# LoRA matmul on one core: the first load moved up in the load queue, and the first store held until most of the first loads have landed

## The chip, the cores and the metric

The kernel runs on one core of one Trainium2 chip. The metric is the device time of one execution in microseconds (us); of several executions the median is taken. A profiled execution also has a span, the time from its first to its last recorded instruction, and its own device time, which is a little longer than the span.

## The reference

`x` has 32768 rows of 256 float32 numbers (a batch of 16 by 2048), `W` is 256 x 256, and the adapter has rank 16. What is computed is

```python
x_flat = x.reshape(-1, in_dim)
y = x_flat @ W
lora_out = x_flat @ lora_A      # 256 x 16
lora_out = lora_out * lora_E    # 16 numbers
lora_out = lora_out @ lora_B    # 16 x 256
y = y + scale * lora_out        # float32, shape of x
```

`x` is 33.6 MB and is read once; the output is as large and is written once. Everything else is small: `W` 256 KB, `lora_A` and `lora_B` 16 KB each, `lora_E` 64 bytes.

## The kernel before

The adapter is folded into the weights once: `weff = W + A diag(E * scale) B`, in bfloat16, and then every row of `x` is multiplied by `weff` alone.

**Chunks and the ring.** `PLAN` cuts the rows into seven chunks of 16, 32, 48, 48, 32, 48 and 32 blocks of 128 rows (a block is 128 KB of `x`, so 2, 4 and 6 MB a chunk). In SBUF they live in `xy`, a ring of `RING` = 176 blocks. The first five chunks (`LEAD`) fill the ring exactly. A chunk's result is written over its own rows in the ring and stored from there, so chunk 5 can be loaded only when the stores of chunks 0 and 1 have landed, and chunk 6 only when that of chunk 2 has.

**SyncE (SP)** issues every transfer of the kernel, on one queue, in an order written out by hand: `W`, `lora_A`, chunk 0, `lora_B`, `lora_E`, chunks 1 to 4 (lines 120 to 126), then chunk by chunk the stores (line 129), each as soon as `s_rdy` says that the chunk is computed. Behind the store of chunk 2 it waits for the stores named in `owners` (line 132) and issues the loads of chunks 5 and 6. At the end it waits for the stores.

**VectorE (DVE)** first makes `ate` (line 170) and `weff` (line 176), then takes the chunks in pieces of 16 blocks: it waits for the chunk's load (`s_in`), casts the piece to bfloat16 (line 184) and copies the transposed blocks from PSUM to SBUF (line 188, twice a piece). At the first piece of chunk `PAUSE` = 4 it also waits until the store of chunk 2 has landed:

```python
            if r == 0 and i == PAUSE:
                dve.wait_ge(s_out[again - 1], 16)
```

`again` is 3 here, so it is the store of chunk 2. The last six evictions of PSUM are VectorE's too (line 154).

**TensorE (PE)** transposes `lora_A` (line 216), multiplies `ate` by `lora_B` (line 220), and waits for `weff` (line 223). Then it loops over the 16 pieces: transposes (line 197), products with `weff` (line 205). **ScalarE (ACT)** evicts the products from PSUM into the ring (line 154) and raises `s_rdy` at the end of a chunk. **GpSimd (POOL)** makes the identity matrix, casts `lora_B` (line 145) and passes on one semaphore per chunk.

Of the kernel before, what the change touches and what calls it, by code (L numbers as in the profile page):

```python
# [6 lines left out]

PLAN = [16, 32, 48, 48, 32, 48, 32]  # L10

RING = 176

LEAD = 5
AFTER = {2: [5, 6]}

PAUSE = 4

# [6 lines left out]
def kernel(  # L25
# [20 lines left out]
    KC = K // P  # L46
    CHUNKS = len(PLAN)
    assert K == M == KC * P and sum(PLAN) * P == N and all(b % G == 0 for b in PLAN)

    def sbuf(name, shape, dt):  # L50
        return ctx.enter_context(nc.sbuf_tensor(name, shape, dt))

    def psum(name, shape, dt):
# [6 lines left out]
    w_sb = sbuf("w_sb", [P, KC, M], FP32)  # L60
    a_sb = sbuf("a_sb", [P, KC, R], FP32)
    b_sb = sbuf("b_sb", [R, M], FP32)
    e_sb = sbuf("e_sb", [R, 1], FP32)
    b_bf = sbuf("b_bf", [R, M], BF16)
    ate = sbuf("ate", [R, KC, P], BF16)
    weff = sbuf("weff", [P, KC, M], BF16)
# [5 lines left out]
    ps_at = ps_y[0][:R, 0, :].rearrange("r (c p) -> r c p", c=KC)  # L72
    ps_aeb = ps_y[1][:, :KC, :]

    sem = tc.alloc_semaphore
    s_w, s_a, s_b, s_e = sem("s_w"), sem("s_a"), sem("s_b"), sem("s_e")
    s_in = [sem(f"s_in{i}") for i in range(CHUNKS)]
    starts = [sum(PLAN[:i]) for i in range(CHUNKS)]
    places = [r % RING for r in starts]
    assert sum(PLAN[:LEAD]) <= RING and all(r + b <= RING for r, b in zip(places, PLAN))  # L80

    owners = {
        i: [j for j in range(LEAD) if places[j] < places[i] + PLAN[i] and places[i] < places[j] + PLAN[j]]
        for i in range(LEAD, CHUNKS)
    }
# [4 lines left out]
    s_lora = sem("s_lora")  # L90
    s_lpe = sem("s_lpe")
# [7 lines left out]
    def rows_of(flat, i):  # L99
        b, r0 = PLAN[i], starts[i] * P  # L100
        return flat[r0:r0 + b * P, :].rearrange("(p b) k -> p b k", b=b)

    def ring_of(i):
        return xy[:, places[i]:places[i] + PLAN[i], :]


    def pieces(rows):
        return [(i, r) for i, b in enumerate(PLAN) for r in range(0, b, rows)]

    def rows_at(i, r, rows):  # L110
        return xy[:, places[i] + r:places[i] + r + rows, :]

    with tc.tile_critical(sync_engine=mybir.EngineType.SP, no_gpsimd_drain=True):  # L113
        sp, pe, dve, act, pool = nc.sync, nc.tensor, nc.vector, nc.scalar, nc.gpsimd


        def load(i):
            sp.dma_start(out=ring_of(i), in_=rows_of(x_flat, i)).then_inc(s_in[i], 16)

        sp.dma_start(out=w_sb[:], in_=W.rearrange("(p c) m -> p c m", c=KC)).then_inc(s_w, 16)  # L120
        sp.dma_start(out=a_sb[:], in_=lora_A.rearrange("(p c) r -> p c r", c=KC)).then_inc(s_a, 16)
        load(0)
        sp.dma_start(out=b_sb[:], in_=lora_B).then_inc(s_b, 16)
        sp.dma_start(out=e_sb[:], in_=lora_E[:, None]).then_inc(s_e, 16)
        for i in range(1, LEAD):
            load(i)
        for i in range(CHUNKS):
            sp.wait_ge(s_rdy, i + 1)
            sp.dma_start(out=rows_of(out_flat, i), in_=ring_of(i)).then_inc(s_out[min(i, again)], 16)
            for later in AFTER.get(i, []):  # L130
                for j in owners[later]:
                    sp.wait_ge(s_out[j], 16)
                load(later)
        for i in range(len(s_out) - 1):
            sp.wait_ge(s_out[i], 16)


        pool.memset(ident[:], 0.0).then_inc(s_id, 1)  # L138
        pool.wait_ge(s_id, 1)
        pool.affine_select(  # L140
            out=ident[:], in_=ident[:], compare_op=mybir.AluOpType.not_equal, fill=1.0,
            base=0, pattern=[[-1, P]], channel_multiplier=1,
        ).then_inc(s_id, 1)
        pool.wait_ge(s_b, 16)
        pool.tensor_copy(out=b_bf[:], in_=b_sb[:]).then_inc(s_lora, 1)  # L145

        copies = pieces(Q)

        def y_of(q, engine, copy):
            i, r = copies[q]
            engine.wait_ge(s_p, q + 1)
            done = copy(out=rows_at(i, r, Q), in_=ps_y[q % 2][:])  # L154
            if r + Q == PLAN[i]:
                done.then_inc(s_rdy, 1)
            else:
                done.then_inc(s_y[q % 2], 1)

        for i in range(CHUNKS - 1):  # L160
            pool.wait_ge(s_rdy, i + 1).then_inc(s_y[((starts[i] + PLAN[i]) // Q - 1) % 2], 1)


        for q in range(len(copies) - LATE):
            y_of(q, act, act.copy)


        dve.wait_ge(s_e, 16)
        dve.wait_ge(s_lpe, 1)
        dve.tensor_scalar(  # L170
            out=ate[:], in0=ps_at, scalar1=e_sb[:], scalar2=float(scale),
            op0=mybir.AluOpType.mult, op1=mybir.AluOpType.mult,
        ).then_inc(s_lora, 1)
        dve.wait_ge(s_w, 16)
        dve.wait_ge(s_lpe, 2)
        dve.tensor_add(out=weff[:], in0=w_sb[:], in1=ps_aeb).then_inc(s_lora, 1)  # L176

        for g, (i, r) in enumerate(pieces(G)):
            if r == 0:
                dve.wait_ge(s_in[i], 16)  # L180
            if r == 0 and i == PAUSE:
                dve.wait_ge(s_out[again - 1], 16)

            dve.tensor_copy(out=xb[:], in_=rows_at(i, r, G)).then_inc(s_xb, 1)  # L184
            for k in range(g * G // S, (g + 1) * G // S):

                dve.wait_ge(s_t, k + 1)
                dve.tensor_copy(  # L188
                    out=xt[k % 2][:].rearrange("w j p c -> w j (p c)"), in_=ps_xt[k % 2][:].bitcast(BF16),
                ).then_inc(s_xt, 1)  # L190
        for q in range(len(copies) - LATE, len(copies)):
            y_of(q, dve, dve.tensor_copy)


        def transposes(k):
            for j in range(S):
                t = pe.transpose(ps_xt[k % 2][:, j, :], xb[:, k * S + j, :].bitcast(FP32), ident[:])  # L197
            t.then_inc(s_t, 1)

        def products(k):  # L200
            for h in range(S // Q):
                pe.wait_ge(s_y[h], 1).then_inc(s_y[h], -1)  # L202
                for j in range(Q):
                    for c in range(KC):
                        m = pe.matmul(  # L205
                            ps_y[h][:, j, :], xt[k % 2][:, h * Q + j, :, c], weff[:, c, :],
                            start=(c == 0), stop=(c == KC - 1),
                        )
                m.then_inc(s_p, 1)

        for h in range(2):
            pe.sem_inc(s_y[h], 1)
        pe.wait_ge(s_a, 16)
        pe.wait_ge(s_id, 2)
        for c in range(KC):
            t = pe.transpose(ps_at[:, c, :], a_sb[:, c, :], ident[:])  # L216
        t.then_inc(s_lpe, 1)
        pe.wait_ge(s_lora, 2)
        for c in range(KC):
            m = pe.matmul(ps_aeb[:, c, :], ate[:, c, :], b_bf[:], start=True, stop=True)  # L220
        m.then_inc(s_lpe, 1)

        pe.wait_ge(s_lora, 3)
        with pe.Fori(0, sum(PLAN) // G):
            pe.wait_ge(s_xb, 1).then_inc(s_xb, -1)  # L225
            for k in range(G // S):
                transposes(k)
            for k in range(G // S):
                pe.wait_ge(s_xt, 1).then_inc(s_xt, -1)
                products(k)  # L230
# [39 lines left out]
```

## Time and profile before

| | |
|---|---|
| median of 3 runs | 165.87 us (165.84, 165.87, 166.8) |
| the profiled execution, its own time | 165.25 us |
| its span | 163.5 us |
| its mean granted TensorE clock | 0.89 |
| TensorE busy (matmul) | 97.1 us, 59% of the span |
| VectorE busy | 81.7 us, 50% |
| ScalarE busy | 57.2 us, 35% |
| bytes moved | 67.42 MB, 412 GB/s over the span |
| time in the packets of SP's queue, as a share of the 16 DMA engines | 96.7% |

Times in the profile are microseconds from the start of the span. The profiled execution took 1.75 us more than its span (165.25 less 163.5), and this part is the same for all that follows. Its own time lies 0.6 us below the median of the runs. The table by stretches gives, for each stretch of the span, the busy time of the engines, then the granted TensorE clock, the share of time that the DMA engines were busy and the rate in GB/s. A packet is one partition's part of a transfer, up to 48 KB; in a stretch of one or two microseconds the rate is coarse, because a whole packet is booked in one place and the share can then pass 1.

### The profile page before, as it was taken

Reading aid. Unit: us, or ns where it says so; the run is one execution under the profiler, and the core shown is the slowest. Engines: PE = TensorE matmul, PEld = TensorE weight load, DVE = VectorE, ACT = ScalarE, POOL = GpSimd, SP = SyncE. Lnnn points to the kernel's source line nnn. Section 1 sums busy time; section 2 is a strip of 40 time slices with the busy share of each in tenths; the row PEclk is TensorE's granted clock in tenths of the full one; section 3 lists DMA queues with packets and bytes.
Section 4 is the critical chain, followed back from the end, with each engine's and each line's share of the span. In section 5 each row is a group of like instructions: output and inputs, shape, how many; then the busy total and the mean of one; then the engine's idle time right before and its main releaser. Section 6 shows DMA issues by size and latency. Waiting matters only on the chain. (4 is left out here: it accounts for less than half of the span.)

```text
span 163.5 us, 1907 instructions
## 1 busy us (share of the span) xinstructions
PE 97.1 (59%) x772; PEld 79.6 (49%) x772; DVE 81.7 (50%) x56; ACT 57.2 (35%) x59; POOL 1.1 (1%) x7
## 2 busy tenths in 40 slices
PE   0014998868978979886000698889789893810000
PEld 0004776747757767674000667677577672600000
DVE  0025768557494684850002484864946849730000
ACT  3000265490844737549000026648457420000000
POOL 1000000000000000000000000000000000000000
PEclk9999999999999999999755569999999998796555
DMA  5999999899999989999999998999998999999991
GB/s 140 401 461 449 449 457 409 385 481 457 409 417 401 377 361 457 457 445 409 457 457 421 397 481 389 425 449 425 469 445 361 457 433 437 493 397 401 425 409 48
DMA packets 2370, 67.42 MB, mean 412 GB/s; under 512 B 432, under 2 KB 448, under 8 KB 576
## 3 DMA queue, kind: packets, MB, share of 16 engines
q1 hardware_dynamic: 2368, 67.40, 96.7%
q14 instruction: 2, 0.02, 0.0%
HBM read 33.85 MB, written 33.55 MB: 412 GB/s over the span
## 5 line engine op out<-in xcount | busy, mean ns | idle before, releaser
L154 ACT COPY xy<-ps_y 128x1024 f32<-128x1024 f32 x58 | 56.0, 1016 | 73.7 <-PE ps_y L205 73.7
L205 PE MATMUL ps_y<-weff,xt 128*128 128x256 bf16 x512 | 64.2, 279 | 16.9 <-PEq L202 16.9
L205 PEld LDWEIGHTS ps_y<-weff,xt 128*128 128x128 bf16 x512 | 48.0, 100 | 32.5 <-issue 24.5
L188 DVE COPY xt<-ps_xt 128x2048 bf16<-128x2048 bf16 x32 | 37.9, 1220 | 32.3 <-PE ps_xt L197 32.3
L184 DVE CAST xb<-xy 128x4096 bf16<-128x4096 f32 x16 | 36.6, 2286 | 18.2 <-DMA out_dram<-xy 15.8
L197 PE MATMUL ps_xt<-ident,xb 128*128 128x128 f32 x256 | 34.1, 292 | 19.1 <-PEq L225 19.1
L197 PEld LDWEIGHTS ps_xt<-ident,xb 128*128 128x128 f32 x256 | 31.4, 151 | 20.3 <-issue 20.1
L154 DVE COPY xy<-ps_y 128x1024 f32<-128x1024 f32 x6 | 7.2, 1220 | 1.4 <-PE ps_y L205 1.3
L170 DVE TENSOR_SCALAR ate<-ps_y,e_sb 16x256 bf16<-16x256 f32 x1 | 0.5, 471 | 10.4 <-DMA e_sb<-in_lora_E_dram 10.4
L220 PE MATMUL ps_y<-b_bf,ate 16*128 16x256 bf16 x2 | 0.6, 402 | 6.5 <-DVE ate L170 6.5
L220 PEld LDWEIGHTS ps_y<-b_bf,ate 16*128 16x128 bf16 x2 | 0.1, 104 | 7.0 <-DVE ate L170 7.0
L216 PE MATMUL ps_y<-ident,a_sb 128*16 128x128 f32 x2 | 0.6, 402 | 3.8 <-DMA a_sb<-in_lora_A_dram 3.8
L216 PEld LDWEIGHTS ps_y<-ident,a_sb 128*16 128x16 f32 x2 | 0.1, 90 | 3.8 <-DMA a_sb<-in_lora_A_dram 3.8
L154 ACT ACT_TABLE_LOAD x1 | 1.3, 1283 | 0.9 <-SPq L113 0.9
L176 DVE TENSOR_TENSOR weff<-w_sb,ps_y 128x512 bf16<-128x512 f32 x1 | 0.7, 686 | 0.8 <-PE ps_y L220 0.8
L145 POOL CAST b_bf<-b_sb 16x256 bf16<-16x256 f32 x1 | 0.4, 386 | 8.6 <-DMA b_sb<-in_lora_B_dram 8.6
L140 POOL TENSOR_SCALAR_AFFINE_SELECT ident<-ident 128x128 f32<-128x128 f32 x1 | 0.3, 292 | 0.2 <-POOL ident L138 0.2
L138 POOL MEMSET ident<- 128x128 f32 x1 | 0.2, 204 | 0.5 <-SPq L113 0.5
L251 POOL MEMSET const-bfloat16-1.0<- 128x1 bf16 x1 | 0.1, 101 | 0.0
L251 POOL MEMSET const-uint8-127<- 128x1 uint8 x1 | 0.1, 101 | 0.0
L251 POOL MEMSET const-float32-0.0<- 128x1 f32 x1 | 0.1, 98 | 0.2 <-issue 0.2
L251 POOL MEMSET const-float32-1.0<- 128x1 f32 x1 | 0.1, 98 | 0.0
## 6 DMA issues: line engine op xcount, KB each, us to landing
xy<-in_x_dram SPq DMA_DIRECT2D x3, 6144.0 KB, 30.6
out_dram<-xy SPq DMA_DIRECT2D x3, 6144.0 KB, 31.1
xy<-in_x_dram SPq DMA_DIRECT2D x3, 4096.0 KB, 24.5
out_dram<-xy SPq DMA_DIRECT2D x3, 4096.0 KB, 30.1
xy<-in_x_dram SPq DMA_DIRECT2D x1, 2048.0 KB, 8.1
out_dram<-xy SPq DMA_DIRECT2D x1, 2048.0 KB, 41.3
w_sb<-in_W_dram SPq DMA_DIRECT2D x1, 256.0 KB, 2.7
a_sb<-in_lora_A_dram SPq DMA_DIRECT2D x1, 16.0 KB, 2.4
```

The costliest lines, as they stand in the source:

```text
L140: pool.affine_select(out=ident[:], in_=ident[:], compare_op=mybir.AluOpType.not_equal, fill=1.0, base=0, pattern=[[-1, P]], channel_multip ...
L145: pool.tensor_copy(out=b_bf[:], in_=b_sb[:]).then_inc(s_lora, 1)
L154: done = copy(out=rows_at(i, r, Q), in_=ps_y[q % 2][:])
L170: dve.tensor_scalar(out=ate[:], in0=ps_at, scalar1=e_sb[:], scalar2=float(scale), op0=mybir.AluOpType.mult, op1=mybir.AluOpType.mult,).the ...
L176: dve.tensor_add(out=weff[:], in0=w_sb[:], in1=ps_aeb).then_inc(s_lora, 1)
L184: dve.tensor_copy(out=xb[:], in_=rows_at(i, r, G)).then_inc(s_xb, 1)
L188: dve.tensor_copy(out=xt[k % 2][:].rearrange("w j p c -> w j (p c)"), in_=ps_xt[k % 2][:].bitcast(BF16),).then_inc(s_xt, 1)
L197: t = pe.transpose(ps_xt[k % 2][:, j, :], xb[:, k * S + j, :].bitcast(FP32), ident[:])
L205: m = pe.matmul(ps_y[h][:, j, :], xt[k % 2][:, h * Q + j, :, c], weff[:, c, :], start=(c == 0), stop=(c == KC - 1),)
L216: t = pe.transpose(ps_at[:, c, :], a_sb[:, c, :], ident[:])
L220: m = pe.matmul(ps_aeb[:, c, :], ate[:, c, :], b_bf[:], start=True, stop=True)
L251: nc = _bacc.Bacc("TRN2", target_bir_lowering=False, num_devices=1)
```

## The change

1. `W` and chunk 0 are issued first; `lora_A`, `lora_B` and `lora_E` follow, then the other first loads.
2. Chunk 4 (32 blocks) is cut into two chunks of 16 blocks. There are now eight chunks, the first six of them fill the ring, and the last two loads are numbered 6 and 7. `PAUSE` stays 4, which is still the same row of `x`.
3. Before SP issues the first store it also waits for the load of chunk `LEAD - 2` = 4, the next to last of the first loads.
4. On VectorE the two instructions that make `ate` and `weff` stand behind the cast of the first piece instead of ahead of it.

```diff
-PLAN = [16, 32, 48, 48, 32, 48, 32]
+PLAN = [16, 32, 48, 48, 16, 16, 48, 32]
 RING = 176
-LEAD = 5
-AFTER = {2: [5, 6]}
+LEAD = 6
+AFTER = {2: [6, 7]}
 PAUSE = 4
...
         sp.dma_start(out=w_sb[:], in_=W.rearrange("(p c) m -> p c m", c=KC)).then_inc(s_w, 16)
+        load(0)
         sp.dma_start(out=a_sb[:], in_=lora_A.rearrange("(p c) r -> p c r", c=KC)).then_inc(s_a, 16)
-        load(0)
         sp.dma_start(out=b_sb[:], in_=lora_B).then_inc(s_b, 16)
         sp.dma_start(out=e_sb[:], in_=lora_E[:, None]).then_inc(s_e, 16)
         for i in range(1, LEAD):
             load(i)
         for i in range(CHUNKS):
             sp.wait_ge(s_rdy, i + 1)
+            if i == 0:
+
+                sp.wait_ge(s_in[LEAD - 2], 16)
             sp.dma_start(out=rows_of(out_flat, i), in_=ring_of(i)).then_inc(s_out[min(i, again)], 16)
...
-        dve.wait_ge(s_e, 16)
-        dve.wait_ge(s_lpe, 1)
-        dve.tensor_scalar(
-            out=ate[:], in0=ps_at, scalar1=e_sb[:], scalar2=float(scale),
-            op0=mybir.AluOpType.mult, op1=mybir.AluOpType.mult,
-        ).then_inc(s_lora, 1)
-        dve.wait_ge(s_w, 16)
-        dve.wait_ge(s_lpe, 2)
-        dve.tensor_add(out=weff[:], in0=w_sb[:], in1=ps_aeb).then_inc(s_lora, 1)
-
         for g, (i, r) in enumerate(pieces(G)):
...
             dve.tensor_copy(out=xb[:], in_=rows_at(i, r, G)).then_inc(s_xb, 1)
+            if g == 0:
+                dve.wait_ge(s_e, 16)
+                dve.wait_ge(s_lpe, 1)
+                dve.tensor_scalar(
+                    out=ate[:], in0=ps_at, scalar1=e_sb[:], scalar2=float(scale),
+                    op0=mybir.AluOpType.mult, op1=mybir.AluOpType.mult,
+                ).then_inc(s_lora, 1)
+                dve.wait_ge(s_w, 16)
+                dve.wait_ge(s_lpe, 2)
+                dve.tensor_add(out=weff[:], in0=w_sb[:], in1=ps_aeb).then_inc(s_lora, 1)
             for k in range(g * G // S, (g + 1) * G // S):
```

## The prediction

> **What bounds the kernel now.** I read the page's DMA part first, then its transfers, then the table by stretches. From the page, the transfer rate and the queue:
>
> ```profile
> DMA  5999999899999989999999998999998999999991
> DMA packets 2370, 67.42 MB, mean 412 GB/s; under 512 B 432, under 2 KB 448, under 8 KB 576
> q1 hardware_dynamic: 2368, 67.40, 96.7%
> ...
> xy<-in_x_dram SPq DMA_DIRECT2D x1, 2048.0 KB, 8.1
> out_dram<-xy SPq DMA_DIRECT2D x1, 2048.0 KB, 41.3
> w_sb<-in_W_dram SPq DMA_DIRECT2D x1, 256.0 KB, 2.7
> a_sb<-in_lora_A_dram SPq DMA_DIRECT2D x1, 16.0 KB, 2.4
> ```
>
> The DMA engines are busy from the second slice of 40 to the last but one; no compute engine passes 59%. So the kernel is its transfers, one behind the other, and a microsecond can come only from the start, the end, or a stretch in which the engines run below their pace. The pace is 433 GB/s (the stretch 10 to 50 us): 67.42 MB take 155.7 us at it, of a span of 163.5. The other 7.8 us are what is to be had.
>
> The store of 2 MB shows the order. It is issued at 23.45 and lands 41.3 later, at 64.75. The table of transfers issued from 4.7 to 5.6 us has chunk 4's load (issued at 5.2):
>
> ```profile
> xy<-in_x_dram SPq DMA_DIRECT2D x1, 6144.0 KB, 44.2
> xy<-in_x_dram SPq DMA_DIRECT2D x1, 4096.0 KB, 54.7
> ```
>
> That load lands at 59.9, and the first store 4.85 us later; 2.10 MB at 433 GB/s are 4.84 us. The store got nothing done before the last of the first loads was through: the queue runs in order of issue. Landings follow in that order at the time their bytes need: chunk 0's load at 9.96, then, from the same view, 19.8, 34.4, 48.9, 59.9, then stores at 64.75, 74.4 and 89.0, the two last loads at 103.4 and 113.5, stores at 127.9, 137.8, 152.5 and 162.2. A step of 6 MB takes 14.4 to 14.7 us and one of 4 MB 9.65 to 10.1. One step stands out: chunk 4's load, 4 MB, takes 11.0 (48.9 to 59.9). The table by stretches shows where:
>
> ```profile
> 3.20:3.60 0.40, 0.00 (x0) 0.00 (x0) 0.00 (x0) 0.00 (x0) 0.00 (x0) 1.00 0.94 249
> 3.60:4.00 0.40, 0.18 (x2) 0.10 (x2) 0.00 (x0) 0.00 (x0) 0.00 (x0) 1.00 0.43 123
> ...
> 10.00:50.00 40.00, 30.47 (x242) 25.12 (x243) 26.42 (x18) 18.05 (x19) 0.39 (x1) 1.00 1.00 433
> ...
> 55.00:56.00 1.00, 1.00 (x11) 0.79 (x10) 0.65 (x1) 0.70 (x2) 0.00 (x0) 1.00 0.77 229
> 56.00:57.00 1.00, 1.00 (x12) 0.94 (x10) 0.00 (x0) 1.00 (x2) 0.00 (x0) 1.00 1.32 393
> 57.00:58.00 1.00, 1.00 (x12) 1.00 (x10) 0.29 (x1) 0.85 (x1) 0.00 (x0) 1.00 0.37 131
> ...
> 110.00:112.00 2.00, 1.68 (x16) 1.29 (x14) 2.00 (x1) 1.90 (x2) 0.00 (x0) 1.00 1.17 500
> 112.00:114.00 2.00, 2.00 (x20) 1.78 (x19) 0.06 (x1) 1.70 (x3) 0.00 (x0) 1.00 0.97 418
> ```
>
> The last two columns are the DMA share and GB/s. Two weak places: a hole at 3.2 to 4.0, just before chunk 0's bytes flow, and a sag from 55 to 58, just before the queue turns from the first loads to the first store: 251 GB/s for 3 us, so 1.26 us lost (3 x 182/433). The other turn from loads to stores, near 112, has no such sag (459 GB/s over 110 to 114). The change touches both weak places.
>
> **The change part by part**, against the profiled execution's 165.25 us.
>
> *Chunk 0 ahead of lora_A.* The issues start at 0.94 (W), 1.38 (lora_A) and 1.86 (chunk 0); chunk 0 moves up by 0.48 us, to 1.38. The hole at 3.6 to 4.0 (share 0.43) says that engines were done with W and lora_A and waited for chunk 0, so an earlier issue fills it. Bounds: 0, if the engine that ends last didn't wait there; 0.48, all of the move. The deficit of the two stretches is nearest: 0.4 x (184 + 310)/433 = 0.46 us. I take **0.4 off**. The bytes of lora_A, lora_B and lora_E are only moved: 32 KB are 0.08 us in either place.
>
> *VectorE's new order.* Nothing of it reaches the end, but it could cost if it delayed the first chunks by tens of microseconds, so here is the count. Chunk 0 lands at about 9.5, and lora_A, lora_B, lora_E right behind, by 10.35 as lora_E does now (2.80 + 7.5). The cast (2.29) runs 9.5 to 11.8 while TensorE transposes lora_A (0.6); `ate` (0.47) to 12.3, the product (0.60 and 0.1 of passing on) to 13.0, `weff` (0.69) to 13.7; the first transposes at about 13.9 instead of 14.62. Chunk 0 is computed some 0.7 us before today's 23.45, and its store now waits for something else: **0**. Its cover is the load queue, full until 59.9; without it the 0.7 us would count.
>
> *Chunk 4 as two.* One load and one store more. Each issue takes 0.33 to 0.45 us on SP, which has time: it stands 88.8 us in waits for ScalarE. In the queue the landings above follow each other without a gap at 2, 4 and 6 MB (the 2 MB store: 4.85 of 4.84), so a cut costs between 0 and 0.1 each; **0.1 on** in all. The 16 rounds of VectorE stay the same, and `PAUSE` is at the same row.
>
> The Trainium skill, page "DMA: Bandwidth & Descriptors", section "Anatomy of one DMA — SWDGE (gpsimd) path", speaks against the cut: a fit of about 2.0 us for each transfer, whatever its size, on top of its bytes. It was made for another issuing path; by it two transfers more would add an estimated 4 us, and the sum would be 169; the same page says that this part overlaps where a transfer is issued early, and the 2 MB store's step agrees.
>
> *The wait ahead of the first store.* With the cut, the load of 16 blocks ahead of the last lands one 2 MB step before 59.5, so near 54.2 (with the 0.4 off and part of the sag; 53.4 without). Behind the waiting store on SP stand the store of chunk 1 (computed at 36.73 today, so it waits too, and goes out 0.4 us after the first) and the store of chunk 2 (computed at 57.88, not held). The two loads behind that wait for landings at 74.4 and 89.0, which follow the queue. When the first store is issued the queue still holds chunk 5's load, 4.84 us of work. The nearest row for how long a fresh transfer takes to move bytes is W: issued 0.94, flowing in the stretch from 2.0, so 1.1 us; lora_A needs 2.4 to land at all. The engine that runs ahead of the others has less cover: the rates after 159 us (164, 66, 0) show that engines end up to about 2 us apart. So 4.84 - 2.0 - 1.1 leaves 1.7 us spare. The wait costs **0** as long as these hold. From then on the queue has 6 MB of stores, 14.5 us, and chunk 2's store joins at about 57.5.
>
> *What the wait does to the sag.* The trace doesn't show what causes it: all I see is that it lies where the first loads end, and that the first two stores (23.45, 36.73) had been queued for a long time, while the load rate stayed 433 with them in the queue. Bounds: 0 (it comes with the turn to the first store, whenever that was issued) and 1.3 off (the 11.0 step becomes 9.7); on the bad side, a second sag of that size when two stores enter the queue at 54 in the midst of a load. I take **0**: the queue's order is unchanged, the stores again stand behind a load when the turn comes, and 30 us of early stores did no harm to the loads.
>
> Sum: 165.25 - 0.4 + 0.1 = 164.95, and 0.3 below the median of the runs is **165.6**. Either differs from the time before by 0.2%; a measurement of this kernel tells it from no change only from about 1% (1.66 us) on.
>
> **The rivals.**
>
> *The sag goes.* For it: it occurs once, at the one turn where stores had waited in the queue for over 20 us; at 112, where the store had been issued at 89.34 behind a load, it doesn't. Against it: the same stores did nothing to 30 us of loads. Price: 1.3 more, 0.3 to 1.7 off in all: 165.87 - 0.3 - 1.3 = 164.3. If the start also gives its whole 0.48, and the sag took more than its mean from the engine that ends last, it reaches 163.8.
>
> *The queue runs dry at the turn (slower).* The wait replaces a queue that always had a store ready by one that must be refilled in 4.84 us. For it: bytes wait for semaphore, issue and first packet in turn; against it: 1.7 us spare by the rows above. It decides from the point where issue to first bytes exceeds 2.8 us (4.84 - 2.0) under a full load. Then the engines stand idle, and each microsecond is one of the time; the price by the nearest rows is 1 to 2.4 (lora_A's whole trip): 166.6 to 168.0, with 167.6 where it is at its full size.
>
> *The change does nothing.* The order of bytes is the same, and if the last engine was never idle at 3.6 us, it is 165.87 give or take the 0.6 by which the profiled execution differs from the median.
>
> **How the numbers follow.** Forecast (small gain, sag stays) 0.47; does nothing 0.18; the sag goes 0.24; queue dry 0.11. Of the sag's case two thirds end beyond 1% faster, since 1.66 off is just at its price (0.15); of the dry queue's, most end over 1% slower (0.09); the rest, 0.76, is within. The range goes from 164.0 (nearly all of the sag's case) to 166.9 (the smaller half of the dry queue, and the scatter of single runs, 166.8).
>
> **What would show it.** Chunk 0's load landing at 9.5 instead of 9.96 and no stretch near 123 GB/s at 3.6: the first term. A first store issued near 54 and landing near 64.4, as before: the wait is free. A stretch of 250 GB/s in the 3 us before the first store's bytes: the sag stayed; a steady 430 there: it went, and the final landing moves up by over 1 us. A DMA share clearly under 0.9 at 58 to 60 with no packets under way: the dry queue. The prediction is wrong if the last landing moves by more than all of these together, for instance if chunks 6 and 7, or the time after the pause at 76 to 89 us, change their place in the queue.

## The result, and the profile after

The changed kernel takes 165.01 us (median of 12 runs, 164.73 to 165.72); the kernel before took 165.98 (12 runs, 165.55 to 166.8) beside it. The ratio is 0.9942, with a 95% interval of 0.9924 to 0.996: 1.0 us faster, which is well clear of the scatter and still within 1%.

The two profiled executions don't show this. The one of before took 165.25 us, that of after 165.35 (span 163.6). Each lies away from the median of its kernel, before's 0.73 below and after's 0.34 above; what the runs show of the reasons stands further down. The comparison rests on the 12 runs of each, and the two traces are read for places, not for the sum.

From the page of after, the transfer rate, the queue and the transfers:

```profile
span 163.6 us, 1911 instructions
...
DMA  5999988998899999999999997999997999989990
DMA packets 2658, 67.42 MB, mean 412 GB/s; under 512 B 464, under 2 KB 480, under 8 KB 608
...
q1 hardware_dynamic: 2656, 67.41, 96.8%
...
w_sb<-in_W_dram SPq DMA_DIRECT2D x1, 256.0 KB, 2.8
a_sb<-in_lora_A_dram SPq DMA_DIRECT2D x1, 16.0 KB, 7.4
```

The queue is still the bound, at 96.8% of the span. lora_A now lands 7.4 us after its issue instead of 2.4, because chunk 0 stands ahead of it. The table of transfers issued between 0.9 and 1.5 us has chunk 0, and that of 53.0 to 53.3 the first store:

```profile
xy<-in_x_dram SPq DMA_DIRECT2D x1, 2048.0 KB, 7.7
...
out_dram<-xy SPq DMA_DIRECT2D x1, 2048.0 KB, 10.0
```

Chunk 0 is issued at 1.38 and lands at 9.08, 0.88 before the 9.96 of before. The first store is issued at 53.03 and lands at 63.0, where it landed at 64.75. SP's own waits show the hold and what stands behind it:

```profile
SPq L131 <- DMA xy<-in_x_dram: 47.2, 1, 47.2
SPq L132 <- ACT xy L157: 39.9, 4, 20.0
SPq L268 <- DMA out_dram<-xy: 17.5, 1, 17.5
```

Line 131 is the new wait: SP stands in it for 47.2 us, and the waits for ScalarE that it takes in drop from 88.8 to 39.9.

The table by stretches, before's two answers first, then after's (the last two columns are DMA share and GB/s):

```profile
2.00:10.00 8.00, 0.59 (x2) 0.10 (x2) 0.00 (x0) 0.18 (x1) 0.00 (x0) 1.00 1.01 384
55.00:58.00 3.00, 3.00 (x29) 2.73 (x28) 0.95 (x2) 2.55 (x3) 0.00 (x0) 1.00 0.82 251
```

```profile
2.00:10.00 8.00, 0.60 (x2) 0.10 (x2) 0.84 (x1) 0.19 (x1) 0.50 (x1) 1.00 1.11 422
3.60:4.00 0.40, 0.00 (x0) 0.00 (x0) 0.00 (x0) 0.00 (x0) 0.00 (x0) 1.00 0.34 123
55.00:58.00 3.00, 2.76 (x25) 2.44 (x24) 1.08 (x1) 1.93 (x2) 0.00 (x0) 1.00 0.97 355
58.00:60.00 2.00, 1.56 (x15) 1.43 (x16) 2.00 (x3) 0.48 (x1) 0.00 (x0) 1.00 1.01 434
```

From 2 to 10 us after moves 38 GB/s more, 0.30 MB in 8 us, which at 433 GB/s is 0.70 us of transfers. The stretch ahead of the first store is weak in both, less so in after. Behind it, at 58 to 60, the share in after is 1.01 at 434 GB/s: the queue did not run dry at the turn.

### The profile page after: what moved, and what is told of

Read it like the earlier page. It is cut to its first block, busy times and chain, and to the rows that moved or that the text cites. A ratio compares the mean times of both kernels' runs of the same rounds, so it can differ in the third digit from the quotient of the medians.

```text
span 163.6 us, 1911 instructions
## 1 busy us (share of the span) xinstructions
PE 96.8 (59%) x772; PEld 79.3 (49%) x772; DVE 81.7 (50%) x56; ACT 57.2 (35%) x59; POOL 2.9 (2%) x7
## 3 DMA queue, kind: packets, MB, share of 16 engines
q1 hardware_dynamic: 2656, 67.41, 96.8%
## 5 line engine op out<-in xcount | busy, mean ns | idle before, releaser
L148 POOL CAST b_bf<-b_sb 16x256 bf16<-16x256 f32 x1 | 2.2, 2196 | 7.8 <-DMA b_sb<-in_lora_B_dram 7.8
```

## The experiments

Two theories were tested first. **S**: the whole gain is the start, and the hold does nothing. **H**: half of it is the start, half is the hold, by taking away the sag ahead of the first store. The first four kernels ran on one chip, beside 23 runs of before (median 165.57).

### The start alone

```diff
-PLAN = [16, 32, 48, 48, 16, 16, 48, 32]
+PLAN = [16, 32, 48, 48, 32, 48, 32]
-LEAD = 6
-AFTER = {2: [6, 7]}
+LEAD = 5
+AFTER = {2: [5, 6]}
...
-            if i == 0:
-
-                sp.wait_ge(s_in[LEAD - 2], 16)
```

(against the changed kernel)

> The seven chunks of before and no hold; only chunk 0 ahead of lora_A and VectorE's new order. Theory S (all of the 0.97 us gain is the start, the sag before the first store is chance): ratio 0.994, about 1.0 us under before. Theory H (half is the start, half is the hold that takes the sag away): 0.4 to 0.5 under before, ratio 0.997; chunk 0's load lands near 9.1 instead of 9.96, and chunk 4's load still takes 11.0 instead of 9.7.

Measured: 164.67 us, ratio 0.9942 (0.9918 to 0.9967), the same as the whole change. Chunk 0 lands at 9.18. The stretch 55 to 58 is as weak as in before:

```profile
55.00:58.00 3.00, 2.78 (x26) 2.46 (x24) 1.06 (x1) 1.93 (x2) 0.00 (x0) 1.00 0.76 246
```

So the sag (the fall in rate ahead of the first store) is there, at 246 GB/s, and the gain is there too: theory S. Chunk 4's load took 10.3 us, not the 11.0 that was expected.

### The cut and the hold alone

```diff
-PLAN = [16, 32, 48, 48, 32, 48, 32]
+PLAN = [16, 32, 48, 48, 16, 16, 48, 32]
-LEAD = 5
-AFTER = {2: [5, 6]}
+LEAD = 6
+AFTER = {2: [6, 7]}
...
+            if i == 0:
+
+                sp.wait_ge(s_in[LEAD - 2], 16)
```

(against the kernel before)

> The start of before; chunk 4 cut in two and the first store held. Theory S: as before within 0.2 us, ratio 1.000. Theory H: 0.5 us under before, ratio 0.997; chunk 0's load lands at 9.96 as before, and the two loads that end the first phase take 9.7 to 10.0 together, with no stretch near 250 GB/s.

Measured: 165.32 us, ratio 0.9995 (0.9966 to 1.0024). Chunk 0 lands at 9.86, and the two loads that end the first phase take 10.9 us together, where one load took 11.0. The hold didn't take the sag away. No gain or loss shows, but the interval reaches down to 0.9966, so this run alone doesn't rule out theory H's 0.997; the next one does.

### The change without the hold

```diff
-            if i == 0:
-
-                sp.wait_ge(s_in[LEAD - 2], 16)
```

(against the changed kernel)

> The changed kernel without the wait ahead of the first store: new start, eight chunks, first store at about 23. Theory S: as after, ratio to before 0.994. Theory H: the sag is back, 1 us before the first store's bytes, ratio 0.997. A third theory, that the cut itself acts (smaller packets at the turn): as after, with no sag although nothing is held.

Measured: 164.62 us, ratio 0.994 (0.9919 to 0.9962), again the whole gain and clear of theory H's 0.997. SP's issues of the stores from the timeline, and the first of them from the transfers issued between 22 and 23 us:

```profile
22.78 34.63 SPq L129 DMA_DIRECT2D out_dram<-xy  x3
...
out_dram<-xy SPq DMA_DIRECT2D x1, 2048.0 KB, 40.2
```

22.78 + 40.2 = 63.0. In after the first store was issued at 53.03 and landed 10.0 later, at 63.0 as well. Thirty microseconds of hold change nothing in when the store lands, because the queue runs in order. The two loads ahead of it take 10.1 us together with or without the hold.

### The hold on the very last load

```diff
-                sp.wait_ge(s_in[LEAD - 2], 16)
+                sp.wait_ge(s_in[LEAD - 1], 16)
```

(against the changed kernel)

> The changed kernel with the first store held until the very last of the first loads has landed (near 58.1 instead of 53.0). The queue must run dry: from the last packet of that load until the first store's bytes, 1.1 (W's issue to first bytes) to 2.4 us (lora_A's whole trip) are lost, plus up to 0.5 that the engine ahead of the others waits longer. So 1.1 to 2.4 us over after: 166.1 to 167.4, ratio to before 1.001 to 1.009. If it equals after, the queue's emptiness costs nothing and the DMA engines aren't the bound at this place.

Measured: 166.79 us, ratio to before 1.0073 (1.0051 to 1.0095), 2.17 us over the kernel without a hold, beside the same runs of before. The stretches around the turn, without a hold first, then with the hold on the last load:

```profile
55.00:57.00 2.00, 2.00 (x20) 1.92 (x20) 0.09 (x1) 1.88 (x2) 0.00 (x0) 1.00 1.06 377
57.00:59.00 2.00, 1.31 (x13) 1.05 (x12) 2.00 (x2) 0.05 (x1) 0.00 (x0) 1.00 0.92 393
```

```profile
55.00:57.00 2.00, 2.00 (x20) 1.92 (x20) 0.11 (x1) 1.90 (x2) 0.00 (x0) 1.00 0.92 393
57.00:59.00 2.00, 1.31 (x13) 1.05 (x12) 2.00 (x2) 0.03 (x1) 0.00 (x0) 1.00 0.31 131
```

The DMA engines stand at a share of 0.31 for 2 us. 262 GB/s less for 2 us are 1.2 us, and the first store lands 1.2 later (57.90 + 6.3 = 64.2 against 63.0). The other 1.0 us is lost behind it: in these two traces the kernel with the hold is 1.4 us late at the landing of the second store, 1.8 at that of the third and 2.2 at the last. Why it falls further behind there was not tested. The queue's emptiness is a price of the size that the rival named, and the change as it stands keeps clear of it.

### Which part of the start

With the gain placed in the start, two causes were left: **I**, chunk 0 is issued one place earlier; **P**, the eight packets of 128 bytes that lora_A puts on each DMA engine hold up what follows. The four kernels of this section ran beside the same runs of before (median 166.28).

```diff
 # swap_only, against the kernel before; nothing else differs
         sp.dma_start(out=w_sb[:], ...)
+        load(0)
         sp.dma_start(out=a_sb[:], ...)
-        load(0)
```

> The kernel before with one line moved: chunk 0 issued ahead of lora_A. VectorE's order, the chunks and the stores are those of before. If the start is the swap of the two issues alone and VectorE's order is covered by the load queue: 0.9 us under before, ratio 0.994, although chunk 0 is computed some 2 us later than in start_only. If VectorE's new order is needed for the gain: about 1.000.

Measured: 164.9 us, ratio 0.9923 (0.9898 to 0.9947). One moved line gives the whole gain. Its chunk 0 (issued at 1.38) has, in the table of transfers issued between 1.3 and 3 us:

```profile
xy<-in_x_dram SPq DMA_DIRECT2D x1, 2048.0 KB, 7.9
```

Chunk 0's cast begins at 12.05 here and at 9.16 in after, and that is worth nothing: VectorE's new order is covered by the queue.

```diff
 # b_between, against the kernel before
-        sp.dma_start(out=a_sb[:], ...)
+        sp.dma_start(out=b_sb[:], ...)
         load(0)
-        sp.dma_start(out=b_sb[:], ...)
+        sp.dma_start(out=a_sb[:], ...)
```

> The kernel before with lora_B instead of lora_A between W and chunk 0, so that chunk 0 is issued at 1.86 as before, but ahead of it stands one 1 KB packet on each DMA engine instead of eight of 128 bytes. Theory I (what counts is that chunk 0 is issued one place earlier): as before, ratio 1.000, chunk 0 landing near 9.9. Theory P (lora_A's many small packets hold up what follows them): as after, ratio 0.994 to 0.996, chunk 0 landing at 9.1 to 9.4.

Measured: 166.49 us, ratio 1.001 (0.9984 to 1.0036). With one packet per engine in lora_A's place the time stays that of before: P falls. Chunk 0 landed at 10.96 (1.86 + 9.1) in the profiled execution, a microsecond later than the 9.9 that theory I gives:

```profile
xy<-in_x_dram SPq DMA_DIRECT2D x1, 2048.0 KB, 9.1
```

```diff
 # later_start, against the kernel before
         sp.dma_start(out=a_sb[:], ...)
-        load(0)
         sp.dma_start(out=b_sb[:], ...)
+        load(0)
```

> The kernel before with chunk 0 issued one place later still, behind W, lora_A and lora_B, at 2.33 instead of 1.86. Theory I: the hole ahead of chunk 0 grows by another 0.47 us, chunk 0 lands near 10.4, ratio 1.003 to 1.005. Theory P: lora_B adds one packet per engine, within 0.1 us of before, ratio 1.000.

Measured: 165.79 us, ratio 0.9976 (0.9957 to 0.9995). A miss for I, and P's 1.000 lies just outside too: one place more in front of chunk 0 costs nothing, and may even save 0.2%. It was run a second time:

> later_start once more, since its 0.9976 fitted neither theory: by chunk 0's landing (10.23 against 9.96) it should be 0.3 us slower than before. If its chance: ratio 1.000 to 1.003. If the order W, lora_A, lora_B, chunk 0 is really better than before's: again 0.996 to 0.999, with chunk 0's last engine closer to the first than in before.

Measured: 165.66 us beside 166.05, ratio 0.9982 (0.9964 to 1.0). It points the same way as the first, though its interval reaches 1.0; a cost of 0.3% or more, which theory I gives, is out in both. Chunk 0 landed at 10.23 and at 10.73 in the two profiles. The first place behind W costs 0.9 us or more, a second one costs nothing more. So neither theory stands as it was put. Not tried was a chunk 0 issued at 1.86 with nothing in front of it but W: without it, the later issue and the small transfer in front are not told apart.

```diff
 # x_first, against the kernel before
+        load(0)
         sp.dma_start(out=w_sb[:], ...)
         sp.dma_start(out=a_sb[:], ...)
-        load(0)
```

> The kernel before with chunk 0 issued as the very first transfer, at 0.94, then W, lora_A, lora_B, lora_E. W's 256 KB (0.6 us at 433 GB/s) then come behind chunk 0, so no byte is saved against swap_only; what can be saved is what is left of the hole. Theory I: within 0.3 us of swap_only, ratio 0.992 to 0.996. If it is clearly under 0.992, the start held more than the swap took out.

Measured: 164.92 us, ratio 0.9917 (0.9892 to 0.9942), as swap_only within 0.1%. Once no small transfer stands between W and chunk 0, no worth of their order shows.

### The hole made large

```diff
 # wait_w, against swap_only
+        sp.wait_ge(s_w, 16)
         load(0)
```

> swap_only with one wait more: chunk 0 is issued only when W has landed, at about 3.75 instead of 1.38. Theory I (an idle DMA engine at the start is carried to the end in full): W's bytes end near 3.2, chunk 0's flow from 3.75 + 1.1 = 4.85, so a hole of 1.6 us where swap_only has none; chunk 0 lands near 10.9, 1.6 after swap_only's 9.3, and the time is 1.4 to 1.8 over swap_only's, ratio to before 1.001 to 1.004. Rival (the hole is made good later, where engines that are behind meet fewer sags): under 0.5 us over swap_only, ratio under 0.996.

Measured: 166.96 us beside 166.05, ratio 1.0059 (1.0037 to 1.0082). Against swap_only, by the two ratios (1.0059 less 0.9923, of 166), that is 2.3 us, with about 0.5 either way from the two intervals; 1.4 to 1.8 were expected. The rival, under 0.5, is out. The stretches, swap_only first, then wait_w:

```profile
2.00:3.00 1.00, 0.00 (x0) 0.00 (x0) 0.00 (x0) 0.19 (x1) 0.00 (x0) 1.00 0.95 236
3.00:4.00 1.00, 0.00 (x0) 0.00 (x0) 0.00 (x0) 0.00 (x0) 0.00 (x0) 1.00 1.35 397
4.00:5.00 1.00, 0.00 (x0) 0.00 (x0) 0.00 (x0) 0.00 (x0) 0.00 (x0) 1.00 0.86 360
```

```profile
2.00:3.00 1.00, 0.00 (x0) 0.00 (x0) 0.00 (x0) 0.19 (x1) 0.00 (x0) 1.00 0.91 238
3.00:4.00 1.00, 0.00 (x0) 0.00 (x0) 0.00 (x0) 0.00 (x0) 0.00 (x0) 1.00 0.05 18
4.00:5.00 1.00, 0.00 (x0) 0.00 (x0) 0.00 (x0) 0.00 (x0) 0.00 (x0) 1.00 1.12 213
```

A hole of a microsecond at 3 to 4, chunk 0 landing at 11.31 (3.61 + 7.7) instead of 9.28 (1.38 + 7.9), 2.03 later where 1.6 was reckoned, and 2.3 us in the time. What the start loses is not made good in the 150 us behind it.

### A second trace of each kernel

> The kernel before, a second trace. If the sag ahead of the first store belongs to this kernel: chunk 4's load again takes 10.3 to 11.0 us instead of 9.7, and chunk 0's load again lands near 9.96 with the hole ahead of it. If it was chance: 9.7 to 9.9.

Measured: 166.17 us for the profiled execution. Chunk 0 landed at 10.66 (1.86 + 8.8), 0.7 later than in the first trace; chunk 4's load took 9.9 us, not 11.0. Chunk 0's row and the stretches:

```profile
xy<-in_x_dram SPq DMA_DIRECT2D x1, 2048.0 KB, 8.8
...
2.00:10.00 8.00, 0.60 (x2) 0.10 (x2) 0.00 (x0) 0.19 (x1) 0.00 (x0) 1.00 0.97 347
55.00:58.00 3.00, 2.68 (x25) 2.26 (x24) 1.29 (x1) 2.70 (x4) 0.00 (x0) 1.00 1.00 366
58.00:60.00 2.00, 1.31 (x13) 1.09 (x12) 1.65 (x2) 0.49 (x1) 0.00 (x0) 1.00 0.79 336
```

The hole at the start is there again, and larger (347 GB/s from 2 to 10, where the first trace had 384). In GB/s the sag is still there, in part moved to 58 to 60 with the later loads (336 there, 410 in the first trace), but it cost the load 0.2 us and not 1.3. So its cost changes from one execution of the kernel to the next. Over all traces this step of 4 MB took 10.35 to 11.0 us in five of the six with a small transfer behind W, and 9.8 to 10.3 in the other eight.

> The changed kernel, a second trace. The loads that end the first phase again take 10.1 together, chunk 0 lands at 9.1 to 9.3; the stretch in which the store of chunk 2 took 15.3 us (73.1 to 88.4) was chance and is back at 14.5 to 14.8, so that the last store lands near 161.5 instead of 162.3.

Measured: 165.17 us. Chunk 0 landed at 9.28, the loads that end the first phase took 9.9 us together, and the store of chunk 2 took 14.7 instead of 15.3: that stretch had been chance. The last store landed at 162.1 (141.83 + 20.3), not at 161.5, so the time won there was lost elsewhere.

### One table from all the traces

When chunk 0 lands, and the same profiled execution's own time. A trace has sixteen landing records for a transfer of this size, as many as there are DMA engines; "first" is the first of chunk 0's, "apart" the time from there to the last, which is its landing (within 0.06 of issue plus trip):

| kernel | chunk 0 issued | first | apart | lands | GB/s, 2 to 10 us | own time | own time less landing |
|---|---|---|---|---|---|---|---|
| no hold | 1.38 | 8.42 | 0.72 | 9.18 | 417 | 164.52 | 155.3 |
| swap only | 1.38 | 8.39 | 0.87 | 9.28 | 413 | 164.82 | 155.5 |
| start only | 1.38 | 8.42 | 0.78 | 9.18 | 417 | 164.91 | 155.7 |
| after, second | 1.38 | 8.48 | 0.76 | 9.28 | 410 | 165.17 | 155.9 |
| after | 1.38 | 8.39 | 0.75 | 9.08 | 422 | 165.35 | 156.3 |
| before | 1.86 | 8.72 | 1.28 | 9.96 | 384 | 165.25 | 155.3 |
| cut and hold only | 1.86 | 8.84 | 1.07 | 9.86 | 380 | 165.31 | 155.5 |
| before, second | 1.86 | 9.21 | 1.46 | 10.66 | 347 | 166.17 | 155.5 |
| lora_B between | 1.86 | 8.90 | 2.03 | 10.96 | 364 | 166.19 | 155.2 |
| later start | 2.33 | 9.36 | 0.84 | 10.23 | 364 | 165.31 | 155.1 |
| later start, second | 2.33 | 9.52 | 1.20 | 10.73 | 356 | 165.69 | 155.0 |
| waits for W | 3.61 | 10.67 | 0.67 | 11.31 | 284 | 167.17 | 155.9 |

(x_first, where W lands behind chunk 0, and the hold on the last load, which adds its own hole, are left out.) The last column lies between 155.0 and 156.3 while the landing goes from 9.1 to 11.3. It also says why the first two traces looked alike: before's was an execution with an early chunk 0 (9.96; its second had 10.66). After's has a slow store of chunk 2, but its second trace, without that, is only 0.18 shorter, so the rest of after's distance from its median is unexplained.

The columns "first" and "apart" divide what the start costs. Right behind W, chunk 0's first record comes at 8.4 to 8.5 and its last 0.7 to 0.9 later. With one small transfer in front (before twice, cut and hold only, lora_B between) the first comes at 8.7 to 9.2, on the mean 0.50 later, about the 0.48 of the issue; the engines then land 1.1 to 2.0 apart, on the mean 0.7 more than right behind W. In later start the first record comes later still (9.36 and 9.52), but the engines are only 0.84 and 1.20 apart (1.28 and 1.46 in before), so the last falls among those of the kernels with one small transfer. That is where the cost of the second place went; why the engines drift apart more in one order than in another is open.

## Why the prediction was right, and where a term was off

It forecast 165.6, 0.3 below the median, within 1%, in a range of 164.0 to 166.9. The time is 165.01, 1.0 below: the side, the class and the range hold; the forecast's gain is a third of the measured one. By the prediction's own bound for the start, 0.48, the time could not have gone below 165.4 (165.87 less 0.48). The range held 165.01 because it was stretched to 164.0 for a rival that didn't come true; that part is luck. The prediction also says that a measurement tells this kernel from no change only from about 1% on; twelve runs of each told 0.6% (0.9924 to 0.996).

- **What bounds it.** Right. The queue runs in order of issue (63.0 for the first store with the hold and without), and what holds up chunk 0 costs about its length: 2.3 us for the hole of wait_w, where chunk 0 lands 2.0 later.
- **Chunk 0 ahead of lora_A, 0.4 off.** The place was right: DMA engines lose time ahead of chunk 0's bytes, and the loss reaches the end. This is the term that was mis-sized. It measured 0.88 in the landing of the two traces, and 0.0077 of 166.28 = 1.3 us in the runs of swap_only, 0.96 in those of start_only. The step that failed is the bound above, "0.48, all of the move": the landing moved further than the issue, because the sixteen engines also land closer together (0.7 to 0.9 apart right behind W, 1.1 to 2.0 with one small transfer in front). The hole ahead of chunk 0 is not simply the issue's delay. With something small behind W, chunk 0's landing scatters between 9.9 and 11.0 at the same issue time (before twice, the cut and hold, lora_B between); right behind W it lies at 9.1 to 9.3. What the swap takes away is the delay of the issue and most of the scatter.
- **The rows the hole was read from.** The stretch of 0.4 us at 123 GB/s is still there in after (3.6 to 4.0, above), and was announced to vanish. Half of chunk 0's packets take 0.61 us or more; in a stretch of 0.4 us the booking of whole packets can make such rows; the 8 us from 2 to 10, 384 against 422, would have shown the loss of bytes, but not its size on the last engine.
- **VectorE's new order, 0.** Right: swap_only has the old one and the whole gain. The times were near: cast at 9.16 to 11.45 (said 9.5 to 11.8), transposes at 13.54 (said 13.9).
- **The cut, 0.1 on.** No cost shows: 0.994 with eight chunks and no hold, 0.9942 with seven, beside the same runs of before, though 0.1 is less than the intervals can tell. The Trainium skill's fixed 2.0 us for a transfer (page "DMA: Bandwidth & Descriptors", section "Anatomy of one DMA — SWDGE (gpsimd) path"), which spoke against the cut, was not seen here on transfers that stand in a full queue: two more of them did not cost the estimated 4 us.
- **The hold, 0.** Right: 0.994 without it, 0.9942 with it, and 0.9995 for cut and hold without the start. The load still queued at the turn, 4.84 us of work, was cover enough; the hold on the last load shows that some cover is needed, since there the queue runs dry and 2.2 us are lost, at the upper end of the 1 to 2.4 named for that rival. How little cover would do was not tested.
- **The sag, 0.** Right that the hold would not touch it: 246 GB/s at 55 to 58 without hold, 10.9 us for the last loads with it. Its price of 1.3 was wrong: the rival takes it that what the sag costs the load is carried to the end. In the second trace of before the load took 9.9 us instead of 11.0, and own time less landing is 155.5 there against 155.3, so the 1.1 us don't show at the end. A rival with 0.24 of the chance stood on one execution's row. What makes the sag is still open. It occurred with stores queued early or late, and in the one kernel that had no store queued at the turn (the hold on the last load, one trace) the last load took its plain 4.9 us.
- **The change does nothing (0.18).** Ruled out by the interval.

## What to carry to other kernels

Where one transfer queue is full from start to end, look at the first microseconds: a small transfer between the first two large ones can cost more than its own issue time (here 0.9 us or more for 0.48), and nothing behind it won that back. Holding a transfer that stands behind others in an in-order queue was worth nothing here, and cost 2.2 us once the queue ran dry; splitting a transfer in the full queue showed no cost. Before a weak stretch of one trace becomes a term or a rival, look for it in a second trace of the same kernel, and see whether it reaches the end.

## What the runs showed that was not expected

**GpSimd beside VectorE.** GpSimd's cast of lora_B, 16 x 256 numbers, took 386 ns in before. In after it runs while VectorE casts chunk 0. From the page of before, then that of after:

```profile
L145 POOL CAST b_bf<-b_sb 16x256 bf16<-16x256 f32 x1 | 0.4, 386 | 8.6 <-DMA b_sb<-in_lora_B_dram 8.6
```

```profile
L148 POOL CAST b_bf<-b_sb 16x256 bf16<-16x256 f32 x1 | 2.2, 2196 | 7.8 <-DMA b_sb<-in_lora_B_dram 7.8
```

It ran from 9.50 to 11.70, VectorE's cast from 9.16 to 11.45. All five profiles with the new order have 2.1 to 2.2 us for it, all nine with the old one 0.39. Here it lies off the path, but the product by lora_B, which needs it, began at 11.89, right behind.

**The second place behind W.** One small transfer between W and chunk 0 costs 0.9 us or more, two cost no more than one (0.9976 and 0.9982 against before). The engines' landings show the two parts, a later first engine and a smaller distance between the engines; no run explains the second.
